# Second passes of overfull expert pairs in two branches, and four modulation groups of the second layer moved behind the first layer's experts

## The chip, the cores and the metric

The kernel runs on one core of a Trainium2 chip. The metric is the time of one execution on the device in microseconds (us); lower is better. The core has a matrix engine (PE, whose weight loads are listed as PEld), a vector engine (DVE), an activation engine (ACT), a general engine (POOL) and a queue that issues most transfers (SP). The engines run their own instruction streams and meet at semaphores. The program has real branches: each engine reads a register and jumps or falls through.

## What is computed

Two layers of a trunk over 512 latent and 256 context tokens of width 1024. Each layer begins with a modulation vector of six parts from the conditioning vectors, normalises and modulates its input, projects it, runs four mixers, projects back, and ends in a mixture of 32 experts. Each token goes to two experts of one group. Cut to what matters here:

```python
for layer in range(DEPTH):                                    # DEPTH = 2
    m_lat = split((c_act @ w_mod[layer] + b_mod[layer]), 6)   # w_mod[layer]: 1024 x 6144
    m_ctx = split(c_ctx_act @ w_mod[layer] + b_mod[layer], 6)
    h = rmsnorm(x) * (1 + scale1) + shift1                    # shift1, scale1: the first two of the six parts
    x = x + gate1 * (mixers(h @ w_in[layer]) @ w_out[layer])
    h = rmsnorm(x) * (1 + scale2) + shift2
    for e in range(32):                                       # each token: two experts of one group
        gu = h[tokens of e] @ w_gu[e]                         # 1024 x 512
        y = (silu(gu[:, :256]) * gu[:, 256:]) @ w_dn[e]       # 256 x 1024
    x = x + gate2 * weighted sum of the two y of a token
```

## The kernel before

**Modulation.** The 6144 outputs are computed in 12 groups of 512. `modulation` (L326) issues for one group two small loads of the bias and two loads of 1 MB of `w_mod`, does 64 matmuls of 128x32 by 128x128 with the conditioning vectors `cT`, adds the bias into `mr` and, for groups 0 to 3, transposes it and copies it into the table `AB` from which the first norm of the layer is modulated. The first layer's groups 0 to 3 are computed at the kernel's start. Its groups 4 to 11 and then groups 0 to 3 of the second layer are yielded by `mods` (L1431) into the last weave of the first layer's mixers. A weave takes turns among generators of program pieces by the shares in `STEPS`; this one holds a recurrence, an attention and `mods`, whose share is the last number of `STEPS[0]`. The second layer's weave holds its own groups 4 to 11.

**Experts.** Experts are handled in 16 pairs, one expert on each half of the partitions. A pair needs six pieces of weights of 1 MB: four of `w_gu` and two of `w_dn`. They are loaded by SP into 18 slots (`wslot`), in turn, and `prefetch` orders a piece as soon as its slot can be reused; a rule "few at a time" (`DEEP` = 4) makes each piece wait until the fourth one before it has landed. For a pair, `block_up` does 32 matmuls (`mm<-w,xT`) and the activation `ac`; `into` transposes the next pair's gathered tokens (`pt`); `block_down` transposes the activation (`po`) and does 16 matmuls (`sc<-w,aT`); `weighted` applies the gates; `scatter` adds the rows to the stream `XA` in memory by an indirect transfer of POOL. Where one expert of a pair has more than 64 tokens, a branch (L2038) behind `weighted` does a second pass, up and down, from the same weights. The register `cregs[p_]` tells which: 0 none, 1 or 2 one half of the pair (`half_swapped`), 3 or more both halves and another gather (`swapped`). So the weights of a pair can only be released behind this branch.

**Between the layers.** A last branch (L2052) holds a loop for experts that are still more overfull. An engine that passes this branch waits at its end for its own outstanding transfers, SP for those of all its eight semaphores. Behind it, `norm1` of the second layer loads six tiles `xn` of the stream (L473), squares each on ACT (L481), forms the reciprocal root on ACT as an exponential of a logarithm (L300, L301), scales on DVE (L487), transposes on PE (L498), modulates on ACT into `htmp` (L505), and splits into a high and a low part on DVE. Chunks of `w_in` (L522) are split likewise, the high part on ACT (L527), the low one on DVE (L531). The projection's matmuls (`pj<-h,w`) need both. A scheduler orders each engine's instructions at build time, so they are not always in the order of the code.

## Time and profile before

| quantity | value |
|---|---|
| time, median of 3 runs | 1741.66 us (1739.35 to 1742.36) |
| time of the profiled execution | 1741.17 us |
| its span, first to last instruction | 1739.4 us |
| mean granted clock of PE | 0.938 |
| busy: PE, DVE, ACT, POOL | 1447.7, 700.0, 536.6, 338.8 us |
| moved by transfers | 366 MB |

The span is 1.8 us shorter than the profiled execution's time. Busy times are unions of an engine's instructions, and the shares differ much between stages: first layer's mixers to about 507 us, its experts from 640 to 915, second layer from 922, its experts from 1455 to 1717. A position "at 656.67" is the time from the span's start.

### The profile page before, as it was taken

To read this page: it belongs to the slowest core of one execution; us is meant where nothing else is said; L and a number is where in the kernel's file an instruction comes from. 1 tells how busy PE (TensorE), PEld (TensorE's weight loads), DVE (VectorE), ACT (ScalarE), POOL (GpSimd) and SP (SyncE) were. 2 spreads that over 40 slices of the span, in tenths; PEclk is the share of its full clock that TensorE was granted. 3 is DMA by queue.
4 is the path that set the end of the run, shared out by engine and by line. 5 is a ranking of instruction groups with operands and counts; after the bars stand their busy time and mean duration, and the time that the engine had idled before them with its cause. 6 is when DMAs were issued, how large, how long until landed. Compare 5 with 4: busy or idle time off the path is not lost. (4 is left out here: it accounts for less than half of the span.)

```text
span 1739.4 us, 26685 instructions
## 1 busy us (share of the span) xinstructions
PE 1447.7 (83%) x10515; PEld 985.1 (57%) x10515; DVE 700.0 (40%) x1415; ACT 536.6 (31%) x1086; POOL 338.8 (19%) x262
## 2 busy tenths in 40 slices
PE   6999999989889848887885989999787775887883
PEld 4888778746669823322234978677366672332221
DVE  5263353477733452211114452635876244111111
ACT  5342453464422220100004442624743121100001
POOL 0022121120102233554430020301111122111100
PEclk9999989999999969999997999989898897999997
DMA  9332411057548599999985332211533598999996
GB/s 319 95 117 69 125 57 34 33 190 245 174 149 230 164 385 327 382 373 386 372 297 144 98 89 72 75 31 56 165 127 119 190 308 328 381 347 368 379 382 236
DMA packets 179833, 366.01 MB, mean 210 GB/s; under 512 B 39673, under 2 KB 90529, under 8 KB 179361
## 3 DMA queue, kind: packets, MB, share of 16 engines
q1 hardware_dynamic: 167440, 335.54, 54.7%
q0 software_dynamic: 9216, 20.99, 4.8%
q10 hardware_dynamic: 2960, 6.58, 1.0%
q8 instruction: 138, 2.26, 0.5%
q14 instruction: 79, 0.64, 0.1%
HBM read 338.48 MB, written 39.65 MB: 217 GB/s over the span
## 5 line engine op out<-in xcount | busy, mean ns | idle before, releaser
L297 PE MATMUL mm<-w,xT 128*64 128x512 f32 (+1 forms) x1120 | 269.5, 591 | 31.8 <-DMA w<-in_moe_w_gu_dram 13.3
L297 PE MATMUL pj<-h,w 128*128 128x256 f32 (+1 forms) x1224 | 228.2, 342 | 0.5 <-DVE u L945 0.3
L297 PEld LDWEIGHTS pj<-h,w 128*128 128x128 f32 x1224 | 190.0, 192 | 28.7 <-issue 5.2
L297 PEld LDWEIGHTS mm<-w,xT 128*64 128x64 f32 x1120 | 89.2, 139 | 188.0 <-issue 138.5
L297 PE MATMUL sc<-w,aT 128*64 128x512 f32 x536 | 131.5, 600 | 19.5 <-ACT aT L1953 16.5
L297 PE MATMUL pj<-w,h 128*128 128x256 f32 x864 | 118.3, 294 | 0.0
L297 PEld LDWEIGHTS pj<-w,h 128*128 128x128 f32 x864 | 111.4, 199 | 3.8 <-issue 3.1
L2013 POOL DMA_INDIRECT XA<-yes,row x32 | 50.9, 1590 | 305.3 <-DVEq L2038 254.1
L1943 ACT ACTIVATE ac<-mm 128x256 f32<-128x256 f32 x32 | 12.3, 383 | 312.0 <-PE mm L297 312.0
L1944 DVE TENSOR_TENSOR ac<-ac,mm 128x256 f32<-128x256 f32 x32 | 13.5, 421 | 226.2 <-ACT ac L1943 226.2
L297 PE MATMUL mm<-w,h 128*128 128x256 f32 x624 | 84.2, 296 | 14.0 <-PEq L1526 6.4
L531 DVE TENSOR_TENSOR w<-w 128x2048 fp32r<-128x2048 f32 (+1 forms) x26 | 58.0, 2230 | 91.3 <-ACT w L527 91.3
L297 PEld LDWEIGHTS sc<-w,aT 128*64 128x64 f32 x536 | 42.3, 136 | 85.7 <-issue 54.7
L297 PEld LDWEIGHTS mm<-w,h 128*128 128x128 f32 x624 | 80.8, 203 | 14.7 <-issue 6.6
L1624 POOL TENSOR_TENSOR xh<-xc,gr 128x512 f32<-128x512 f32 (+1 forms) x25 | 30.2, 1208 | 194.2 <-DVE xc L1620 89.7
L297 PE MATMUL sc<-h 128*128 128x256 f32 (+3 forms) x144 | 60.2, 535 | 8.8 <-ACT um L1221 7.8
L1927 PEld LDWEIGHTS pt<-masks,xgr 128*128 128x128 f32 x256 | 28.8, 147 | 68.1 <-issue 68.1
L1927 PE MATMUL pt<-masks,xgr 128*128 128x128 f32 x256 | 40.7, 293 | 31.5 <-DMA xgr<-XG,row 18.0
L527 ACT ACTIVATE w<-w 128x2048 fp32r<-128x2048 f32 (+1 forms) x26 | 48.0, 1847 | 60.6 <-PE pj L297 36.8
L297 PE MATMUL x<-u 64*32 64x32 f32 (+5 forms) x944 | 54.0, 251 | 12.0 <-DVE u L785 9.6
L297 PE MATMUL sc<-h,w 128*128 128x512 f32 (+1 forms) x312 | 59.4, 350 | 0.3 <-ACT ux L300 0.3
L297 PEld LDWEIGHTS x<-u 64*64 64x64 f32 (+4 forms) x944 | 45.4, 146 | 24.3 <-issue 9.1
(399 smaller groups left out, 2367.8 us busy)
## 6 DMA issues: line engine op xcount, KB each, us to landing
w<-in_moe_w_gu_dram SPq DMA_DIRECT2D x128, 1024.0 KB
w<-in_moe_w_dn_dram SPq DMA_DIRECT2D x64, 1024.0 KB
w<-in_w_mod_dram SPq DMA_DIRECT2D x40, 1024.0 KB
w<-in_w_in_dram SPq DMA_DIRECT2D x22, 1024.0 KB
wm<-in_w_mod_dram SPq DMA_DIRECT2D x8, 1024.0 KB
XG<-xh ACTq DMA_DIRECT2D x10, 512.0 KB
w<-in_w_out_dram SPq DMA_DIRECT2D x8, 512.0 KB
w<-in_w_out_dram SPq DMA_DIRECT2D x16, 256.0 KB
```

The lines of the kernel that those rows point to most:

```text
L297: TE.matmul(o, lhsT, rhs, start=start, stop=stop, **kw)
L527: sp = S.activation(hi[:, :, 0:o], raw[:, :, 0:o], AF.Copy)
L531: V.tensor_tensor(lo[:, :, 0:o], raw[:, :, 0:o], hi[:, :, 0:o].bitcast(F32), op=ALU.subtract)
L1624: G.tensor_tensor(xh[:, t0 - qt0:t0 - qt0 + m].rearrange("p n (e c q) -> p c n q e", e=2, c=4)[:, c], xs.rearrange(pairs, e=2), bc(gr[:, 1 ...
L1927: TE.transpose(pt[:, u * P:(u + 1) * P], xg[:, o:o + P], ident)
L1943: S.activation(ac[rs_], pm[rs_, 0:256], AF.Silu)
L1944: V.tensor_tensor(ac[rs_], ac[rs_], pm[rs_, 256:512], op=ALU.mult)
L2013: G.indirect_dma_start(out=XA, out_offset=bass.IndirectOffsetOnAxis(ap=row, axis=0), in_=ye, in_offset=None, bounds_check=T - 1, oob_is_er ...
```

## The change

The four groups of the second layer leave `mods`, and the share of `mods` in that weave goes from 12 to 8. The function `mod_ahead` loads them at the end of the first layer's expert loop: when the loop comes to its last two pairs it takes nine more of the expert slots, one for the four groups' biases (cleared by DVE, filled by eight small loads) and eight for the weights. The matmuls are done behind the last branch (now L2094) by `drain(modulation(...))`. Secondly, the second pass of an overfull pair stands in two branches: its up part directly behind `block_up`, its down part where the whole pass stood. Its activations are kept in `yes` buffers between the two. The diff, cut to its core:

```diff
-STEPS = ((38, 24, 60, 18, 12, 12, 66, 72, 12), (38, 24, 60, 18, 12, 12, 66, 72, 8))
+STEPS = ((38, 24, 60, 18, 12, 12, 66, 72, 8), (38, 24, 60, 18, 12, 12, 66, 72, 8))
...
-    def modulation(L, gs, slot=None, bank=None):
+    def mod_bias(L, g, bt):
+        for w in range(2):
+            nc.sync.dma_start(bt.rearrange("(j r) c -> j r c", r=32)[:, w, :],
+                              a["b_mod"][L, g * 512:(g + 1) * 512].rearrange("(j c) -> j c", j=4))
+    def mod_weights(L, g, kh, wt):
+        nc.sync.dma_start(wt, a["w_mod"][L, kh * 512:(kh + 1) * 512, g * 512:(g + 1) * 512].rearrange("(k p) c -> p k c", p=P))
+    def modulation(L, gs, slot=None, bank=None, there=None):
...
-            bt = bmt[i_ % 4]
-            for w in range(2):
-                nc.sync.dma_start(bt.rearrange("(j r) c -> j r c", r=32)[:, w, :], a["b_mod"][L, cs].rearrange("(j c) -> j c", j=4))
+            bt = there[g][2] if there else bmt[i_ % 4]
+            if not there:
+                mod_bias(L, g, bt)
...
-                    wt = (slot or ring)([P, 4, 512])
-                    nc.sync.dma_start(wt, a["w_mod"][L, k * P:(k + 4) * P, cs].rearrange("(k p) c -> p k c", p=P))
+                    if there:
+                        wt = there[g][k // 4]
+                    else:
+                        wt = (slot or ring)([P, 4, 512])
+                        mod_weights(L, g, k // 4, wt)
                 for j in range(4):
                     mm(pm[32 * j:32 * j + 32, 0:P], cT[:, k, :], wt[:, k % 4, j * P:(j + 1) * P], k == 0, k == KT - 1)
...
         def mods():
             yield from modulation(L, range(4, 12))
-            if not last:
-                yield from modulation(L + 1, range(4))
         weave((hgrn_, st[6]),
               (chain(mla_qkv(Em, hu, cs, c2, mw, mr_), restore(Ex), mla(Em, mr_)), st[7]), (mods(), st[8]))
...
+        ahead = {}
+        def mod_ahead(g):
+            if not ahead:
+                bs = wslot()
+                V.memset(bs[:, 0:512], 0.0)
+                for g_ in range(4):
+                    ahead[g_] = [None, None, bs[:, g_ * P:(g_ + 1) * P]]
+                    mod_bias(L + 1, g_, ahead[g_][2])
+            for kh in range(2):
+                ahead[g][kh] = wslot().rearrange("p (k c) -> p k c", k=4)
+                mod_weights(L + 1, g, kh, ahead[g][kh])
...
-        def half_swapped(p_, wh, xT, ye, gt, h):
+        def half_up(wh, xT, ac, h):
...
+        def half_down(p_, wh, ac, ye, gt, h):
...
+        def overfull(c_, first, second, more):
+            with tc.If(c_ > 0):
+                with tc.If(c_ < 2) as c1_:
+                    first()
+                with c1_.Else():
+                    with tc.If(c_ < 3) as c2_:
+                        second()
+                    with c2_.Else():
+                        more()
...
         xT = block_in(xgs[0], None, (S.copy, S.copy))
         for p_ in range(NP):
             prefetch(max(0, min(6 * p_ + NW, 3 * NEXP) - len(loaded)), False)
+            for g in () if last else range(4):
+                if 6 * p_ + NW >= 3 * NEXP + 2 * g + 3 and (not ahead or ahead[g][0] is None):
+                    mod_ahead(g)
             w_ = pair(p_)
             xT_, ac = xT, block_up(w_, xT)
+            a2, a3 = (yes[:, (p_ + i) % YE, 0:256] for i in (1, 2))
+            def more_up():
+                block_up(w_[::-1], xT_, ac=a2)
+                gather(yes[:, (p_ + 2) % YE], tab(1, p_, "row"))
+                block_up(w_, into(p_, 1, xT_), ac=a3)
+            def more_down():
+                swapped(p_, w_, a2, ye, gt)
+                y1 = block_down(w_, block_act(a3))
+                scatter(weighted(p_ + 1, y1, gates_of(tab(1, p_, "own")), tab(1, p_, "gws")), tab(1, p_, "row"))
             if p_ == 0:
                 slot_weights(ohs, tabs[0])
                 slot_weights(slot_table(wk, 1, tabs[1]["row"]), tabs[1])
+            overfull(cregs[p_], lambda: half_up(w_[0], xT_, a2, 1), lambda: half_up(w_[1], xT_, a2, 0), more_up)
             rows(p_ + NG)
             if p_ + 1 < NP:
                 xT = into(p_ + 1)
             gt = gates_of(tab(0, p_, "own"))
             ye = weighted(p_, block_down(w_, block_act(ac)), gt, tab(0, p_, "gws"))
-            with tc.If(cregs[p_] > 0):
-                with tc.If(cregs[p_] < 2) as c1_:
-                    half_swapped(p_, w_[0], xT_, ye, gt, 1)
-                with c1_.Else():
-                    with tc.If(cregs[p_] < 3) as c2_:
-                        half_swapped(p_, w_[1], xT_, ye, gt, 0)
-                    with c2_.Else():
-                        swapped(p_, w_, xT_, ye, gt)
-                        gather(yes[:, (p_ + 2) % YE], tab(1, p_, "row"))
-                        y1 = block_down(w_, block_act(block_up(w_, into(p_, 1, xT_))))
-                        scatter(weighted(p_ + 1, y1, gates_of(tab(1, p_, "own")), tab(1, p_, "gws")), tab(1, p_, "row"))
+            overfull(cregs[p_], lambda: half_down(p_, w_[0], a2, ye, gt, 1), lambda: half_down(p_, w_[1], a2, ye, gt, 0), more_down)
             scatter(ye, tab(0, p_, "row"))
...
-            pieces[0] = 6
+            pieces[0] = 6 if last else 3 * NEXP + 9
...
                     scatter(weighted(b, y1, gates_of(g_.get("own")), g_["gws"]), g_["row"])
+        if not last:
+            drain(modulation(L + 1, range(4), None, pmm, ahead))
         ec.close()
```

On SP, the last pieces of the first layer's experts and what follows them. Before, the last pieces are two `w_dn` loads; a wait for `DMAHW1` is one for the landing of the latest transfer on that one of SP's eight semaphores, which it uses in turn:

```order
L1465 DMA w_15411<-in_moe_w_gu_dram 128x2x1024 [waits DMAHW1_49,PE_49]
L1465 DMA w_15413<-in_moe_w_gu_dram 128x2x1024 [waits DMAHW2_49,PE_49]
L1470 DMA w_15415<-in_moe_w_dn_dram 128x2x1024 [waits DMAHW3_49]
L1470 DMA w_15417<-in_moe_w_dn_dram 128x2x1024 [waits DMAHW4_49]
L2038 COMPARE_AND_BRANCH
```

After them SP came to the branch L2052. In the changed kernel the same four pieces of the last pair (the last `w_dn` with the wait for `DMAHW4`, the fourth transfer before it; in turn it uses `DMAHW0` itself) are followed by one of the pair's branches and then by these rows, where `w_15450` is the slot of the biases:

```order
L328 DMA w_15450<-in_b_mod_dram 4x128 [waits DVE_49,PE_49]
L328 DMA w_15450<-in_b_mod_dram 4x128 x3
L328 DMA w_15450<-in_b_mod_dram 4x128 [waits DMAHW5_49]
L328 DMA w_15450<-in_b_mod_dram 4x128 [waits DMAHW6_49]
L328 DMA w_15450<-in_b_mod_dram 4x128 [waits DMAHW7_49]
L328 DMA w_15450<-in_b_mod_dram 4x128 [waits DMAHW0_49]
L332 DMA w_15460<-in_w_mod_dram 128x4x512 [waits DMAHW1_49]
```

A further branch follows, and then:

```order
L332 DMA w_15462<-in_w_mod_dram 128x4x512 [waits DMAHW2_49]
L332 DMA w_15464<-in_w_mod_dram 128x4x512 [waits DMAHW3_49]
L332 DMA w_15466<-in_w_mod_dram 128x4x512 [waits DMAHW4_49,PE_49]
L332 DMA w_15688<-in_w_mod_dram 128x4x512 [waits DMAHW5_49]
L332 DMA w_15690<-in_w_mod_dram 128x4x512 [waits DMAHW6_49,PE_49]
L332 DMA w_15692<-in_w_mod_dram 128x4x512 [waits DMAHW7_49]
L332 DMA w_15694<-in_w_mod_dram 128x4x512 [waits DMAHW0_49,PE_49]
L2094 COMPARE_AND_BRANCH
```

What moved: eight small loads and eight of 1 MB stand between the last expert piece and the last branch, and the eighth small load waits for `DMAHW0`. Behind the last branch SP went on before with:

```order
L2052 UNCONDITIONAL_BRANCH [waits DMAHW0_49,DMAHW1_49,DMAHW2_49,DMAHW3_49,DMAHW4_49,DMAHW5_49,DMAHW6_49,DMAHW7_49]
L522 DMA w<-in_w_in_dram 128x8x64 [waits DMASW4_49,DMASW5_49,DMASW0_49,DMASW7_49,DVE_49,DMAHW1_49,PE_49,Pool_49]
L522 DMA w<-in_w_in_dram 128x8x32 [waits DMAHW2_49]
L522 DMA w<-in_w_in_dram 128x8x32 [waits DMAHW3_49]
L473 DMA xn_17222<-XA 128x1024 [waits DMAHW4_49,DMASW3_49]
L473 DMA xn_17229<-XA 128x1024 [waits DMAHW5_49]
L522 DMA w<-in_w_in_dram 128x8x256 [waits DMAHW6_49]
L473 DMA xn_17237<-XA 128x1024 [waits DMAHW7_49]
```

and now with:

```order
L2094 UNCONDITIONAL_BRANCH [waits DMAHW0_49,DMAHW1_49,DMAHW2_49,DMAHW3_49,DMAHW4_49,DMAHW5_49,DMAHW6_49,DMAHW7_49]
L484 DMA xn_17208<-XA 128x1024 [waits DMAHW1_49,DMASW7_49,DMAHW2_49,DMASW3_49,PE_49]
L484 DMA xn_17215<-XA 128x1024 [waits DMAHW3_49,PE_49]
L484 DMA xn_17223<-XA 128x1024 [waits DMAHW4_49,PE_49]
L484 DMA xn_17231<-XA 128x1024
L484 DMA xn_17339<-XA 128x1024 [waits DMAHW5_49]
L533 DMA w<-in_w_in_dram 128x8x64 [waits DMASW5_49,DMASW7_49,DMASW1_49,DMAHW6_49,DVE_49,Pool_49]
L533 DMA w<-in_w_in_dram 128x8x32 [waits DMAHW7_49]
L533 DMA w<-in_w_in_dram 128x8x32 [waits DMAHW0_49]
L484 DMA xn_17347<-XA 128x1024 [waits DMAHW1_49]
L533 DMA w<-in_w_in_dram 128x8x256 [waits DMAHW2_49,PE_49]
```

What moved: the tiles of the stream `xn` stand ahead of the chunk of `w_in`; the wait at the branch's end is the same in form.

On ACT, the start of the second layer. Before:

```order
L527 ACTIVATE w<-w 128x8x128 [waits DMAHW5_49,DMAHW3_49,DMAHW7_49,DMAHW2_49,DMAHW1_49]
L191 ACT_TABLE_LOAD
L481 ACTIVATE junk,ss<-xn_17222 128x1024 [waits DMAHW4_49,DMAHW6_49,DMAHW0_49,PE_49]
L300 ACTIVATE ss<-ss,eps 128x1 [waits Activation_49]
L481 ACTIVATE junk,ss<-xn_17229 128x1024 [waits DMAHW5_49]
L301 ACTIVATE ss<-ss 128x1 [waits Activation_49]
L300 ACTIVATE ss<-ss,eps 128x1 [waits Activation_49]
L301 ACTIVATE ss<-ss 128x1 [waits Activation_49]
L527 ACTIVATE w<-w 128x2048 [waits DMAHW6_49,Pool_49]
L481 ACTIVATE junk,ss<-xn_17237 128x1024 [waits DMAHW7_49]
L505 ACTIVATE htmp<-mm,AB_150 128x256 [waits PE_49]
```

In the changed kernel ACT begins the second layer with the same squares, and these are the first rows and those that follow on them:

```order
L492 ACTIVATE junk,ss<-xn_17208 128x1024 [waits DMAHW3_49,DMAHW2_49,DMAHW4_49,DMAHW1_49,DMAHW6_49,DMAHW0_49,PE_49]
L300 ACT_TABLE_LOAD
L300 ACTIVATE ss<-ss,eps 128x1 [waits Activation_49]
L492 ACTIVATE junk,ss<-xn_17215 128x1024 [waits DMAHW2_49]
L301 ACT_TABLE_LOAD
L301 ACTIVATE ss<-ss 128x1 [waits Activation_49]
L300 ACT_TABLE_LOAD
L300 ACTIVATE ss<-ss,eps 128x1 [waits Activation_49]
L492 ACTIVATE junk,ss<-xn_17223 128x1024 [waits DMAHW3_49]
L301 ACT_TABLE_LOAD
L301 ACTIVATE ss<-ss 128x1 [waits Activation_49]
L300 ACT_TABLE_LOAD
```

```order
L300 ACTIVATE ss<-ss,eps 128x1 [waits Activation_49]
L492 ACTIVATE junk,ss<-xn_17231 128x1024 [waits DMAHW4_49]
L301 ACT_TABLE_LOAD
L301 ACTIVATE ss<-ss 128x1 [waits Activation_49]
L516 ACTIVATE htmp<-mm,AB_150 128x256 [waits DMAHW7_49,DMAHW5_49,PE_49]
L516 ACTIVATE htmp<-mm,AB_150 128x256 [waits PE_49] x3
L516 ACTIVATE htmp<-mm,AB_150 128x256 [waits DVE_49,PE_49,Activation_49] x2
L300 ACT_TABLE_LOAD
L300 ACTIVATE ss<-ss,eps 128x1
L516 ACTIVATE htmp<-mm,AB_150 128x256 [waits DVE_49,PE_49,Activation_49]
L538 ACTIVATE w<-w 128x8x128 [waits DMAHW6_49,DMAHW7_49,DMAHW5_49,DMAHW0_49]
```

What moved: the first `htmp` stands behind four squares and six table loads, one for each change between L300 and L301, where there was one table load before; the split of `w_in` (now L538, followed by one more table load) stands behind seven `htmp`, where it stood first.

On PE, one pair's branch. Before, behind the down matmuls, with the up and the down part inside:

```order
L297 MATMUL sc<-w_14237,aT 64x512
L2016 TENSOR_LOAD cnti
L2038 COMPARE_AND_BRANCH
L2039 COMPARE_AND_BRANCH
L297 MATMUL mm<-w_14227,xT 64x256 x8
L297 MATMUL mm<-w_14231,xT 64x256 x8
L1951 MATMUL po<-masks,ac 128x64 x2
L297 MATMUL sc<-w_14235,aT 64x512 x4
L2039 UNCONDITIONAL_BRANCH
```

In the changed kernel the first branch of a pair, behind its up matmuls, and the second one, behind its down matmuls:

```order
L297 MATMUL mm<-w_15222,xT 64x512
L297 MATMUL mm<-w_15224,xT 64x512
L2053 TENSOR_LOAD cnti
L2038 COMPARE_AND_BRANCH
L2039 COMPARE_AND_BRANCH
L297 MATMUL mm<-w_15218,xT 64x256 x8
L297 MATMUL mm<-w_15222,xT 64x256 x8
```

```order
L297 MATMUL sc<-w_15226,aT 64x512
L297 MATMUL sc<-w_15228,aT 64x512
L2038 COMPARE_AND_BRANCH
L2039 COMPARE_AND_BRANCH
L1975 MATMUL po<-masks,yes 128x64 x2
L297 MATMUL sc<-w_15226,aT 64x512 x4
L2039 UNCONDITIONAL_BRANCH
```

What moved: a pair has two branches to pass. By the code, a pair without a second pass jumps over 152 matmuls and their weight loads before, and over 104 and then 48 now.

## Rows read from the trace of the kernel before

**Rows 1.** The page's head and TensorE's busy time.
```profile
span 1739.4 us, 26685 instructions
...
PE 1447.7 (83%) x10515; PEld 985.1 (57%) x10515; DVE 700.0 (40%) x1415; ACT 536.6 (31%) x1086; POOL 338.8 (19%) x262
```

**Rows 2.** Windows; us, busy (count) of five engines, clock, DMA share, GB/s.
```profile
5.00:30.00 25.00, 14.66 (x179) 10.42 (x179) 13.21 (x47) 16.51 (x44) 0.00 (x0) 1.00 1.04 337
426.00:507.00 81.00, 72.53 (x963) 53.87 (x961) 48.70 (x111) 35.05 (x85) 7.67 (x6) 0.98 0.46 155
650.00:658.00 8.00, 7.45 (x53) 3.58 (x51) 2.88 (x9) 0.48 (x2) 1.08 (x1) 1.00 0.25 64
668.00:684.00 16.00, 13.31 (x60) 4.78 (x58) 2.62 (x4) 1.34 (x3) 12.41 (x6) 0.89 0.99 328
700.00:900.00 200.00, 162.11 (x724) 61.96 (x722) 33.24 (x51) 16.73 (x38) 92.36 (x45) 0.99 1.03 378
1462.00:1474.00 12.00, 10.88 (x76) 4.57 (x74) 3.88 (x16) 1.34 (x3) 2.48 (x2) 1.00 0.39 131
```

**Rows 3.** Windows, matmuls with cT alone; us, busy of PE, PEld, DVE.
```profile
426.00:507.00 81.00, 12.54 (x384) 10.12 (x384) 0.00 (x0) 0.98 0.46 155
```

**Rows 4.** Timeline of SP, start of the first layer's experts.
```profile
656.67 5.83 SPq L1465 DMA_DIRECT2D w<-in_moe_w_gu_dram  x4
...
676.50 2.82 SPq L1465 DMA_DIRECT2D w<-in_moe_w_gu_dram  x4
```

**Rows 5.** Timeline of PE there.
```profile
640.76 7.45 PE L297 MATMUL mm<-w,xT 128*64 128x512 f32 x30
...
654.74 3.62 PE L297 MATMUL mm<-w,xT 128*64 128x256 f32 x32
...
676.68 8.71 PE L297 MATMUL mm<-w,xT 128*64 128x512 f32 x32 [2.17 <-PEq L2038]
```

**Rows 6.** Line of the branch of the second pass; ns min/median/max.
```profile
L2038 PEldq COMPARE_BRANCH  x32: 65/3036/4998, 651.7 to 1713.0; - x32
...
L2038 POOLq INC_SWDGE_SEM  x29: 307/942/1415, 672.9 to 1701.6; - x29
```

**Rows 7.** Timeline of PE, start of the second layer's experts.
```profile
1457.15 7.60 PE L297 MATMUL mm<-w,xT 128*64 128x512 f32 x32
```

**Rows 8.** Timeline of SP there.
```profile
1471.50 1.40 SPq L1465 DMA_DIRECT2D w<-in_moe_w_gu_dram  x3
```

**Rows 9.** Line of the last branch; ns min/median/max.
```profile
L2052 SPq EVENT_SEMAPHORE  x16: 3/17/17, 906.0 to 1712.9; - x16
```

**Rows 10.** Waits of SP between the layers; us, times, longest.
```profile
SPq L522 <- remote: 15.5, 1, 15.5
SPq L2052 <- SPq L2052: 9.4, 1, 9.4
```

**Rows 11.** Timeline of SP between the layers.
```profile
922.43 1.78 SPq L522 DMA_DIRECT2D w<-in_w_in_dram  x3
924.32 1.27 SPq L473 DMA_DIRECT2D xn<-XA  x2
```

**Rows 12.** Timeline of SP at the kernel's start.
```profile
22.50 1.30 SPq L332 DMA_DIRECT2D bmt<-in_b_mod_dram  x2
```

**Rows 13.** Timeline of ACT between the layers.
```profile
927.39 1.06 ACT L527 ACTIVATE w<-w 128x1024 fp32r<-128x1024 f32 x1 [16.91 <-DMA w<-in_w_in_dram]
928.46 1.28 ACT L191 ACT_TABLE_LOAD   x1
929.90 1.06 ACT L481 ACTIVATE junk<-xn 128x1024 f32<-128x1024 f32 x1 [0.16 <-DMA xn<-XA]
...
931.09 0.29 ACT L300 ACTIVATE ss<-ss,eps 128x1 f32<-128x1 f32 x1
...
936.97 0.55 ACT L505 ACTIVATE htmp<-mm,AB 128x256 f32<-128x256 f32 x1
```

**Rows 14.** Timeline of PE there.
```profile
939.90 1.42 PE L297 MATMUL pj<-h,w 128*128 128x256 f32 x5
```

More of the change, by code (lines that the diff above doesn't have):

```diff
@@ L1929, in block_in, with block_up @@
             return xT
+        ahead = {}
[9 more added lines that the diff above has]
+                mod_weights(L + 1, g, kh, ahead[g][kh])
         def span(hv):
             return slice(64 * hv[0], 64 * hv[-1] + 64)
-        def block_up(w_, xT, hv=(0, 1)):
+        def block_up(w_, xT, hv=(0, 1), ac=None):
             pm = pmm()
@@ L1940, in block_up @@
                     mm(pm[hs, :], xT[:, k, hs], w_[h][k // 4][:, k % 4, :], k == 0, k == KT - 1)
-            ac = wk.tile([P, 256], F32, name="ac", tag="ac", bufs=1)
+            if ac is None:
+                ac = wk.tile([P, 256], F32, name="ac", tag="ac", bufs=1)
             rs_ = span(hv)
@@ L1982, in weighted, with swapped @@
             return ye
-        def swapped(p_, w_, xT, ye, gt):
-            y2 = weighted(p_ + 1, block_down(w_[::-1], block_act(block_up(w_[::-1], xT))), gt, tab(0, p_, "swp"))
+        def swapped(p_, w_, ac, ye, gt):
+            y2 = weighted(p_ + 1, block_down(w_[::-1], block_act(ac)), gt, tab(0, p_, "swp"))
             V.tensor_tensor(ye, ye, y2, op=ALU.add)
-        def half_swapped(p_, wh, xT, ye, gt, h):
+        def half_up(wh, xT, ac, h):
             hs, other = span([h]), span([1 - h])
@@ L1995, in half_swapped @@
                     mm(pm[ps, 0:256], xT[:, k, hs], wh[k // 4][:, k % 4, c * 256:(c + 1) * 256], k == 0, k == KT - 1)
-            ac = wk.tile([P, 256], F32, name="ac", tag="ac", bufs=1)
             S.activation(ac[hs], pm[other, 0:256], AF.Silu)
             V.tensor_tensor(ac[hs], ac[hs], pm[hs, 0:256], op=ALU.mult)
+        def half_down(p_, wh, ac, ye, gt, h):
+            hs, other = span([h]), span([1 - h])
             aT = block_act(ac, (h,))
```

## Prediction

> **What bounds the kernel now.** I read the page first: PE is busy for 1447.7 of 1739.4 us [rows 1], so over the whole run PE work taken away looks like time won. That share is a mean over stages, so I next asked for windows, one for each stage that the change touches, and compared in each PE's busy time with the share and rate of the transfers [rows 2]. The last weave of the first layer (426 to 507 us) has PE busy for 72.53 of 81 us and transfers at 0.46: PE nearly sets its pace. The first layer's experts (700 to 900 us) have transfers at a share of 1.03 and 378 GB/s, while PE is busy for 162.11 of 200 us: the loading of weights sets the pace there, and PE work or PE waits in it cost nothing so long as PE keeps up. Two short windows within the expert stages show transfers nearly idle: 650 to 658 us at 64 GB/s, and 1462 to 1474 us at 131 GB/s, while PE is busy in both. There the queue has nothing to load, because no slot is free. Last I followed SP, ACT and PE through the gap between the layers [rows 9 to 14], where PE waits for the stream's tiles and then for ACT's chain until its dense stretch begins at 939.90.
>
> **1. Work taken out of the weave.** Six groups of modulation are done in 426 to 507 us: 384 matmuls with 12.54 us of PE [rows 3], so 2.09 us for a group and 8.4 us for the four that leave. If PE set the pace alone, 8.4 us would be won; if the recurrence beside it did, nothing. PE's share there is 72.53/81 = 0.90, near the first end, and 0.90 x 8.4 = 7.5; I take 6.5, since the shorter queue at the weave's end has less to fill waits with. The eight loads that leave are cover for nothing (share 0.46). **-6.5 (0 to -8.4).**
>
> **2. Slots free earlier at the start of the first layer's experts.** Pair 0's up matmuls end at 640.76 + 7.45 = 648.2 [rows 5], but the first refill is issued at 656.67 [rows 4], because the second pass of this pair (32 matmuls, 654.74, 3.62 us) reads the same weights behind the down matmuls. Now it follows the up directly: 648.2 + 3.6 and about 1 us of activation, then the branch's end, so about 653, 3.7 us earlier. At 378 GB/s as the full rate, the window 650 to 658 lost 8 x (1 - 64/378) = 6.6 us. The window 668 to 684 lost 16 x (1 - 328/378) = 2.1 us: there SP gave out no load until 676.50, when PE had passed the branch of pair 1 (PE waits 2.17 us for it at 676.68). The up of a pair ends some 7 us before that branch, so this second hole should close. I take 3.7 + 2.1, **-6 (-3 to -8.7, all of both holes).** Since transfers pace the rest of the stage, the earlier stream carries through to its end.
>
> **3. The same in the second layer.** Pair 0's up ends at 1457.15 + 7.60 = 1464.75 [rows 7], the first refill is issued at 1471.50 [rows 8], and the window 1462 to 1474 lost 12 x (1 - 131/378) = 7.8 us. No second pass is taken there; with up to 2 us for the added branch the refill goes out at about 1467. **-4.5 (-2 to -7.8).**
>
> **4. The start of the second layer.** This is the dear part, in two steps.
>
> *The stream's tiles.* Before, SP passes the branch when the last expert piece has landed: it comes there at 896.6, waits 9.4 us, and its first semaphore comes at 906.0 [rows 9, 10]. It then waits 15.5 us more for the scatters, and issues at 922.43 the chunk of `w_in` and at 924.32 the tiles [rows 11]; the first square begins at 929.90 [rows 13]. Now eight bias loads and eight weight loads stand on SP ahead of the branch. The eighth bias load uses the semaphore of the last expert piece, so it waits until that has landed, and all the weight loads are queued behind it. So none of the 8.39 MB moves beside the experts. From 906.0 (all in the time of before; part 2's gain shifts both): a bias load takes 1.30/2 = 0.65 us to issue [rows 12], which puts the first weight load at 906.75. A tile takes 929.9 - 924.3 = 5.6 us to land with about 1 MB moved by then, which at 378 GB/s is 2.8, so some 2.8 us are latency. The loads take 8.39 MB at 378 (expert pieces) to 337 GB/s (5 to 30 us, mostly loads of `w_mod`) [rows 2], 22.2 to 24.9, I take 23.5; and 1.5 for the last pair's scatter that shares them. That is 906.75 + 2.8 + 23.5 + 1.5 = 934.5. SP waits for all of it at the branch's end, and only then issues the tiles, which land 4 us later (they now go first; between 1.4 us for 0.5 MB alone and 5.6): 938.7 instead of 929.9, **+8.8**.
>
> *ACT's chain.* Before, the split of the first chunk of `w_in` is done ahead of the tiles (927.39, 1.06 us, then a table load of 1.28); the first `htmp` comes at 936.97 and PE is dense at 939.90, 10.0 us after the first square [rows 13, 14]. Now ACT has, from the first square on: four squares with read-out at 931.09 - 929.90 = 1.2 us, six small operations at some 0.25, six table loads of 1.28, together 14.0; then seven `htmp` at 0.5 (0.55 less overlap), another table load and a small operation, 1.5, the split, 1.06, and DVE's half of it, about as long, 1.2: 7.3. So 21 us instead of 10, **+11**. The four groups' matmuls (8.4 us of PE) run while the weights land and in this chain, and cost nothing; uncovered they would add 8.4.
>
> Together **+20 (+14 to +24)**: the low end has tiles 3 us sooner and 3 us of the chain overlapped, the high end the slow rate and the full 5.6 us of landing.
>
> **5. More branches.** A pair passes two. On the engines other than PE a branch takes some 50 ns; POOL's bookkeeping at it takes 0.94 us in the median and up to 1.42 towards the end [rows 6], and the last scatter is on the path to the end. I take **+1.5 (0 to +2.5)**.
>
> **Sum.** -6.5 - 6 - 4.5 + 20 + 1.5 = +4.5 on the profiled execution's 1741.2, so 1745.7; that execution lies 0.5 below the median of the runs, and I say **1746**. All ends at once give 1730 to 1762.
>
> **Rivals.** *The holes close and the gap hides more (faster).* If transfers run on without a hole in both expert stages, parts 1 to 3 give 8.4 + 8.7 + 7.8 = 25, and the sum is 1741.2 - 25 + 20 + 1.5 = 1738; with the low end of part 4, 1732. For it: PE is ahead of the weights in both starts. Against: the slots of the down weights still wait for the down part, and the first four of six pieces last only some 10 us. It decides from 17 us won in parts 1 to 3 and a part 4 under 14.
>
> *The sum is nil (same).* The terms of both signs are of one size, so 3 us less in part 4, or more in parts 1 to 3, gives 1739 to 1745.
>
> *Both branches stall PE (much slower).* PE's branch takes 3.04 us in the median and up to 5.0 [rows 6], the others' some 50 ns. In 700 to 900 us PE works 162.11 of 200, so 13.8 of a pair's 17 us (six pieces of 1.05 MB at 378 GB/s are 16.6). One stall is covered: of pair 1's, PE sat idle for 2.17 [rows 5]. Two would leave it idle for 4.4, or for 6 with less queued behind it, so 18 to 20 us for a pair: 1.5 to 3 us over, in the 16 of 32 pairs above the median +24 to +48, 1770 to 1794. Against: a jump is now over 104 or 48 matmuls, not 152, and the shortest branch took 65 ns. The Trainium skill ("Runtime: NRT & Kernel Launch", "Instruction fetch mechanics") says that a taken branch stalls when its target is outside a window of two pages of 256 instructions; with their weight loads the jumps are 304 instructions before and 208 and 96 now, so by it stalls become rarer, and the sum stays.
>
> *Table switches cost more than their row (slower).* If the engine empties at each of the seven added switches ahead of the first projection for as long as a load takes, part 4 is +29 and the time 1755. Against: the load at 928.46 begins as the split ends, and the square behind it starts at 929.90 after 0.16 us of idle, put down to the tile [rows 13]; that is 1.28 with no room for more. The Trainium skill ("ScalarE: Activation LUTs", "What ACT_TABLE_LOAD costs") gives 1283 ns and a drain of 1380 ns for every switch, by which the time would be 1755; this trace shows the first and not the second.
>
> **How the numbers follow.** About 0.2%, 3.5 us, is what a measurement of this kernel tells from no change: 1738.2 to 1745.1 is "same". Forecast (slower, 1745 to 1758): 0.39. Nil: 0.28. Faster: 0.25. Stalls 0.04, dear switches 0.04. So faster 0.25, same 0.28, slower 0.47. The range leaves out the stalls, the lowest fifth or so of the faster case and the high end of part 4: 1733 to 1758; the likeliest case alone has 1745 to 1758.
>
> **What would show it.** Right: four groups fewer in 426 to 507; refills at about 653 and 1467 in place of 656.67 and 1471.50 (less what the weave gave); the first added load of `w_mod` issued only as the last `w_dn` lands; the first square 9 us later after that landing than before, PE dense 21 us after the square. Wrong: weight loads of `w_mod` beside the last experts, tiles issued before all of them have landed, holes that stay where they are, or a PE branch above 2 us twice in a pair with transfers falling under 370 GB/s.

## The result, and the profile after

The changed kernel takes 1756.03 us (median of 4 runs, 1751.90 to 1756.32) against 1741.26 for the kernel before (4 runs): a ratio of 1.0074, 95% interval 1.0053 to 1.0096, so 0.7% slower. The forecast was 1746, slower, with 1733 to 1758 as the range. The profiled execution grew from 1741.17 to 1756.09, by 14.9 where the sum of the prediction says +4.5.

The page's head and PE's busy time, as in [rows 1]; PE is busy for 13.5 us more, though it does the same 10515 matmuls, at a mean granted clock of 0.920 in place of 0.938:

```profile
span 1754.2 us, 27020 instructions
...
PE 1461.2 (83%) x10515; PEld 1009.0 (58%) x10515; DVE 702.7 (40%) x1416; ACT 545.0 (31%) x1093; POOL 339.2 (19%) x262
```

To find where the time went I cut every profiled execution at the same six events of its timelines: A, from the start to the first up matmul of the first layer's pair 0; B, to the end of the last down matmul there; C1, to ACT's first square of the second layer; C2, to the 121st projection matmul `pj`; D, to the first up matmul of the second layer; E, to the end. In us (an ordinary table, worked out from starts and ends in the timelines; the experiments stand in it too):

| kernel | A | B | C1 | C2 | D | E | span |
|---|---|---|---|---|---|---|---|
| before | 639.9 | 274.4 | 15.7 | 29.3 | 498.0 | 282.2 | 1739.4 |
| after | 628.7 | 270.7 | 26.8 | 44.3 | 501.0 | 282.5 | 1754.2 |
| e1_split_only | 637.9 | 269.3 | 16.4 | 27.9 | 496.5 | 281.6 | 1729.6 |
| e2_ahead_only | 631.4 | 282.4 | 24.9 | 42.7 | 500.0 | 282.7 | 1764.1 |
| e3_table_once | 626.9 | 269.4 | 28.3 | 44.4 | 495.5 | 283.7 | 1748.2 |
| e4_bias_early | 630.6 | 296.2 | 16.7 | 29.4 | 492.5 | 281.6 | 1747.1 |
| e5_in_order | 631.7 | 277.0 | 22.3 | 29.5 | 498.0 | 281.3 | 1739.8 |
| e6_two_groups | 637.5 | 277.1 | 16.2 | 28.6 | 494.7 | 283.2 | 1737.3 |
| e7_chunks_first | 624.2 | 271.6 | 40.6 | 32.2 | 494.2 | 282.1 | 1744.9 |
| e8_quarter_loads | 631.3 | 268.8 | 13.1 | 44.8 | 499.6 | 277.9 | 1735.5 |
| e9_groups_left_out | 632.0 | 276.4 | 15.7 | 28.7 | 498.8 | 340.7 | 1792.4 |

Each row is one execution. Kernels with the same code in a stage differ there: A by up to 7.8 us (624.2 to 632.0), D by 8.5, E by 2.4 (without e8 and e9, which do other work there). So small differences count only where several rows agree.

After against before: A wins 11.2, B 3.7; C1 loses 11.1, C2 15.0, D 3.0, E nothing. So the loss is the gap between the layers, C1 and C2, 26.1 us.

*The gap, SP.* The timeline of SP there, which answers to [rows 9 to 11] (start, us, then operation, tile and count):

```profile
881.76 10.04 SPq L328 DMA_DIRECT2D w<-in_b_mod_dram  x8
891.84 18.14 SPq L332 DMA_DIRECT2D w<-in_w_mod_dram  x8
922.40 2.26 SPq L484 DMA_DIRECT2D xn<-XA  x5
924.90 6.18 SPq L533 DMA_DIRECT2D w<-in_w_in_dram  x3
931.12 0.96 SPq L484 DMA_DIRECT2D xn<-XA  x1
932.19 25.81 SPq L533 DMA_DIRECT2D w<-in_w_in_dram  x2
```

Its waits, and the windows that go with them (us, busy and count of PE, PEld, DVE, ACT, POOL, granted clock, DMA share, GB/s):

```profile
SPq L2094 <- SPq L2094: 11.6, 1, 11.6
```

```profile
638.89:646.89 8.00, 6.91 (x56) 4.01 (x54) 2.10 (x9) 1.33 (x3) 1.08 (x1) 1.00 0.47 164
656.89:672.89 16.00, 14.01 (x66) 5.84 (x64) 2.67 (x5) 1.31 (x3) 12.55 (x7) 1.00 1.02 368
885.00:892.00 7.00, 7.00 (x34) 2.32 (x34) 2.73 (x3) 0.58 (x1) 1.45 (x2) 1.00 0.38 144
900.00:922.00 22.00, 10.79 (x239) 8.49 (x243) 1.81 (x9) 0.00 (x0) 1.58 (x1) 0.84 0.95 332
939.00:957.00 18.00, 12.54 (x55) 9.99 (x55) 11.22 (x25) 15.86 (x30) 0.00 (x0) 0.59 0.00 1
945.73:970.57 24.84, 22.59 (x144) 21.22 (x144) 11.48 (x27) 13.03 (x28) 0.00 (x0) 0.79 0.15 43
1476.48:1488.48 12.00, 10.00 (x70) 4.17 (x68) 3.38 (x16) 1.34 (x3) 0.99 (x1) 1.00 0.60 210
```

The eight bias loads hold SP for 10 us. The first load of `w_mod` goes out at 891.84; the transfers run nearly dry before it (885 to 892 at 144 GB/s) and carry the 8.39 MB behind it (900 to 922 at 332). SP waits 11.6 us at the branch's end for all of it, and only then, at 922.40, issues the tiles.

*The gap, ACT and PE.* The timelines of ACT and of PE, answering to [rows 13, 14]:

```profile
926.25 1.06 ACT L492 ACTIVATE junk<-xn 128x1024 f32<-128x1024 f32 x1 [30.59 <-DMA xn<-XA]
...
927.42 1.28 ACT L300 ACT_TABLE_LOAD   x1
928.71 0.29 ACT L300 ACTIVATE ss<-ss,eps 128x1 f32<-128x1 f32 x1
...
939.79 2.89 ACT L516 ACTIVATE htmp<-mm,AB 128x256 f32<-128x256 f32 x6
...
944.64 1.04 ACT L538 ACTIVATE w<-w 128x1024 fp32r<-128x1024 f32 x1
...
952.09 0.37 ACT L1280 COPY ux<-pj 128x256 f32<-128x256 f32 x1 [2.04 <-PE pj L297]
...
953.36 1.92 ACT L538 ACTIVATE w<-w 128x2048 fp32r<-128x2048 f32 x1
```

```profile
945.73 0.80 PE L297 MATMUL pj<-h,w 128*128 128x256 f32 x2 [0.47 <-ACT w L538]
946.99 5.06 PE L297 MATMUL pj<-h,w 128*128 128x256 f32 x22 [0.47 <-DVE w L542]
951.85 2.12 PE L509 MATMUL mm<-masks,xn 128*128 128x128 f32 x9
955.33 0.74 PE L297 MATMUL pj<-h,w 128*128 128x256 f32 x4 [1.36 <-ACT w L538]
```

The first `pj` comes 945.73 - 926.25 = 19.5 us after the first square. Before, it came 8.7 us after it (929.90), as PE's timeline and the window up to the 121st `pj` there show:

```profile
938.61 0.79 PE L297 MATMUL pj<-h,w 128*128 128x256 f32 x2
```

```profile
938.61:959.17 20.56, 20.42 (x153) 19.64 (x151) 12.19 (x37) 12.98 (x34) 0.00 (x0) 0.90 0.16 52
```

PE then does 24 `pj` and stands again at 955.33, for the split of the second chunk of `w_in`. That chunk was ordered at 932.19, 9.8 us after the first tile; before it was 1.3. But it isn't the chunk that is late: from 939 to 957 the transfers run at 1 GB/s, so it had landed by then. ACT splits it only at 953.36, behind a copy of the first products (`ux`, 952.09) for which it waits 2.04 us for PE. From the first to the 121st `pj` it takes 24.84 us, before 20.56: PE is idle for 2.25 us in place of 0.14, and busy for 22.59 in place of 20.42, at a mean granted clock of 0.79 in place of 0.90.

*The expert stages.* PE's and SP's timelines at the two starts, answering to [rows 4, 5, 7, 8]; the first line is of the kernel before, where the window of [rows 5] cut off the first two of the 32 matmuls:

```profile
639.85 8.36 PE L297 MATMUL mm<-w,xT 128*64 128x512 f32 x32
```

```profile
628.74 8.57 PE L297 MATMUL mm<-w,xT 128*64 128x512 f32 x32
...
640.07 3.67 PE L297 MATMUL mm<-w,xT 128*64 128x256 f32 x32 [0.24 <-issue]
...
1471.63 8.67 PE L297 MATMUL mm<-w,xT 128*64 128x512 f32 x32
```

```profile
642.05 3.04 SPq L1474 DMA_DIRECT2D w<-in_moe_w_gu_dram  x4
...
1483.50 2.44 SPq L1474 DMA_DIRECT2D w<-in_moe_w_gu_dram  x3
```

The first refill goes out 642.05 - 628.74 = 13.3 us after the first up matmul (656.67 - 639.85 = 16.8 before) and 1483.50 - 1471.63 = 11.9 in the second layer (14.4 before). In windows at the same distance from the first up matmul as those of [rows 2], the hole of 64 GB/s has become 164, that of 131 has become 210, and the 328 at pair 1 has become 368. So the first holes are shorter, not closed.

### The profile page after: what moved, and what is told of

Same layout as the page of the kernel before. It is cut to its first block, busy times and chain, and to the rows that moved or that the text cites. A ratio compares the mean times of both kernels' runs of the same rounds, so it can differ in the third digit from the quotient of the medians.

```text
span 1754.2 us, 27020 instructions
## 1 busy us (share of the span) xinstructions
PE 1461.2 (83%) x10515; PEld 1009.0 (58%) x10515; DVE 702.7 (40%) x1416; ACT 545.0 (31%) x1093; POOL 339.2 (19%) x262
## 5 line engine op out<-in xcount | busy, mean ns | idle before, releaser
L297 PE MATMUL mm<-w,xT 128*64 128x512 f32 (+1 forms) x1120 | 286.9, 598 | 28.7 <-DMA w<-in_moe_w_gu_dram 23.8
L297 PEld LDWEIGHTS mm<-w,xT 128*64 128x64 f32 x1120 | 98.2, 141 | 202.1 <-issue 154.9
L297 PE MATMUL sc<-w,aT 128*64 128x512 f32 x536 | 135.9, 626 | 12.3 <-ACTq L2038 9.0
L1968 DVE TENSOR_TENSOR ac<-ac,mm 128x256 f32<-128x256 f32 x32 | 13.4, 420 | 241.6 <-ACT ac L1967 241.6
L297 PEld LDWEIGHTS sc<-w,aT 128*64 128x64 f32 x536 | 47.3, 143 | 75.1 <-issue 54.5
L297 PEld LDWEIGHTS mm<-w,h 128*128 128x128 f32 x624 | 81.0, 203 | 14.4 <-issue 6.2
L1853 POOL DMA_INDIRECT xgr<-XG,row x32 | 34.5, 1079 | 175.5 <-PE po L1975 98.6
L538 ACT ACTIVATE w<-w 128x2048 fp32r<-128x2048 f32 (+1 forms) x26 | 48.0, 1847 | 41.4 <-PE pj L297 37.1
L297 PEld LDWEIGHTS x<-u 64*32 64x32 f32 (+4 forms) x944 | 46.6, 151 | 24.3 <-issue 15.2
L1936 PE MATMUL pt<-masks,xgr 128*128 128x128 f32 x256 | 37.7, 293 | 21.9 <-DMA xgr<-XG,row 18.3
```

Of the source, the lines that this page charges most:

```text
L297: TE.matmul(o, lhsT, rhs, start=start, stop=stop, **kw)
L538: sp = S.activation(hi[:, :, 0:o], raw[:, :, 0:o], AF.Copy)
L1853: return G.indirect_dma_start(out=xg, out_offset=None, in_=XG, in_offset=bass.IndirectOffsetOnAxis(ap=row, axis=0), bounds_check=T - 1, oo ...
L1936: TE.transpose(pt[:, u * P:(u + 1) * P], xg[:, o:o + P], ident)
L1968: V.tensor_tensor(ac[rs_], ac[rs_], pm[rs_, 256:512], op=ALU.mult)
```

## The experiments

The edits are shown against the changed kernel, that of e9 against the kernel before. Times are medians, ratios are to the kernel before on the same chip.

**One part at a time.** First the split branches without the groups behind the experts:

```diff
-STEPS = ((38, 24, 60, 18, 12, 12, 66, 72, 8), (38, 24, 60, 18, 12, 12, 66, 72, 8))
+STEPS = ((38, 24, 60, 18, 12, 12, 66, 72, 12), (38, 24, 60, 18, 12, 12, 66, 72, 8))
...
             yield from modulation(L, range(4, 12))
+            if not last:
+                yield from modulation(L + 1, range(4))
...
-            for g in () if last else range(4):
-                if 6 * p_ + NW >= 3 * NEXP + 2 * g + 3 and (not ahead or ahead[g][0] is None):
-                    mod_ahead(g)
...
-        if not last:
-            drain(modulation(L + 1, range(4), None, pmm, ahead))
```

> The second passes split in two branches, the modulation left where it was. Theory (the loss lies between the layers, and the split pays a little in both expert stages): about 3.5 us won at the first layer's expert stage and 0 to 3 at the second's, so 1736 to 1740. Rival (the added branches, or the split, cost time themselves): 1745 or more.

Measured: 1733.12 us, ratio 0.9954 (0.9942 to 0.9967): faster, the best version of all, and better than both ranges. B is 5.1 us shorter than before, and in the window at the same distance from the first up matmul (648.08 to 656.08) the transfers run at 156 GB/s in place of 64. E is 0.6 shorter, which is nothing.

Then the groups behind the experts with the second pass in one branch, as before:

```diff
-            overfull(cregs[p_], lambda: half_up(w_[0], xT_, a2, 1), lambda: half_up(w_[1], xT_, a2, 0), more_up)
...
-            overfull(cregs[p_], lambda: half_down(p_, w_[0], a2, ye, gt, 1), lambda: half_down(p_, w_[1], a2, ye, gt, 0), more_down)
+            with tc.If(cregs[p_] > 0):
+                with tc.If(cregs[p_] < 2) as c1_:
+                    half_swapped(p_, w_[0], xT_, ye, gt, 1)
...
```

> The four groups moved behind the first layer's experts, one branch per pair as before. Theory: the weave wins about 11 us, the gap between the layers costs 22 to 26 more, and nothing of the split's gain is there, so 1755 to 1760. Rival (the loss comes from the split): about 1741 or less.

Measured: 1763.07 us, ratio 1.0104 (1.0062 to 1.0147). Its C1 and C2 are as long as in the changed kernel (67.6 against 71.1, before 45.0), so the loss in the gap belongs to the groups. The time is 3 us above the range of the theory. The two parts add up: 21.7 slower and 8.3 faster than the kernel before make 13.4, and the whole change has 0.74% of 1741, 12.9. The 8.5 us that A wins here are lost again in B (8.0 longer); why B is longer without a second branch was not followed further.

**ACT's chain.** One table load ahead of the squares in place of one at each change, and the splits after the third tile:

```diff
+                if n == 0:
+                    ln_exp(x_[0:1, 0:1])
+                fixed(S.activation(junk, x_, AF.Square, accum_out=ss))
...
+                if n == 2 and chunks:
+                    chunks()
...
-            ws_.append(wchunk(C2, first=True))
-            ln_exp()
-            ws_.append(wchunk([(C_G, 256)]))
-            norm1(E, hsplit, early)
+            norm1(E, hsplit, early, lambda: (ws_.append(wchunk(C2, first=True)), ws_.append(wchunk([(C_G, 256)]))))
```

> The changed kernel with one table load ahead of the first square in place of eight between squares, logarithms, exponentials and the split, and the split behind three squares; the loads of w_mod as they were. Theory (ACT's chain is on the path): the dense stretch of PE begins 8 to 11 us sooner behind the first square, 1745 to 1748. Rival (something else, such as the weights of w_in, ends the wait as late): 1754 to 1757.

Measured: 1753.50 us, ratio 1.0072 (1.0045 to 1.0100), against the kernel before the same as the change (1.0074), and just under the rival's range. ACT's chain did become short, but C2 stays at 44.4. PE's and ACT's timelines of this kernel and a window of it show where the time went:

```profile
934.82 0.51 PE L297 MATMUL pj<-h,w 128*128 128x256 f32 x2 [0.62 <-ACT w L542]
...
936.31 4.24 PE L297 MATMUL pj<-h,w 128*128 128x256 f32 x22 [0.71 <-DVE w L546]
942.82 0.80 PE L297 MATMUL pj<-h,w 128*128 128x256 f32 x2 [2.27 <-ACT w L542]
945.15 4.87 PE L297 MATMUL pj<-h,w 128*128 128x256 f32 x22 [1.53 <-DVE w L546]
952.88 1.69 PE L513 MATMUL mm<-masks,xn 128*128 128x128 f32 x6 [2.86 <-DVE xn L502]
```

```profile
940.59 0.37 ACT L1284 COPY ux<-pj 128x256 f32<-128x256 f32 x1 [5.37 <-PE pj L297]
940.86 1.91 ACT L542 ACTIVATE w<-w 128x2048 fp32r<-128x2048 f32 x1
```

```profile
936.00:941.00 5.00, 4.24 (x22) 4.04 (x22) 1.52 (x5) 0.41 (x2) 0.00 (x0) 0.66 0.00 0
```

The first `pj` comes 10.2 us after the first square (924.64) in place of 19.5. Then PE waits for the second chunk's two splits (2.27, 1.53) and for the next tile (2.86). The chunk is there again: nothing is moved from 936 to 941. Its split stands on ACT behind the copy `ux`, for which ACT waits 5.37 us until PE has done its first 24 `pj`. So a second wait in ACT's order takes the place of the first. C1 is no shorter (28.3).

The other order, both chunks split ahead of the squares:

```diff
+                ld = nc.sync.dma_start(xn[n], x_src(L, n))
+                if L:
+                    fixed(ld)
...
+                sq = S.activation(junk, x_, AF.Square, accum_out=ss)
+                if L:
+                    fixed(sq)
...
+                if first:
+                    fixed(ld)
...
-            ws_.append(wchunk([(C_G, 256)]))
+            ws_.append(wchunk([(C_G, 256)], first=True))
```

> The changed kernel with ACT held to the order of before at the second layer's start: both chunks' splits and the one table load ahead of the squares; SP still issues the tiles ahead of the chunks. Theory (in the changed kernel two things end late, ACT's chain by 10.7 us and the second chunk by 4.4 more): the splits wait for the second chunk, which lands some 12 us behind the first tile, then the dense stretch has no gaps; 3 to 6 us less, 1750 to 1753. Rival (ACT's order alone makes the 15 us): 1740 to 1743.

Measured: 1755.93 us, ratio 1.0061 (1.0037 to 1.0085), no better than the change within the intervals, and above both ranges. ACT's timeline:

```profile
930.36 1.06 ACT L544 ACTIVATE w<-w 128x1024 fp32r<-128x1024 f32 x1 [38.31 <-DMA w<-in_w_in_dram]
931.43 1.28 ACT L191 ACT_TABLE_LOAD   x1
934.59 1.91 ACT L544 ACTIVATE w<-w 128x2048 fp32r<-128x2048 f32 x1 [1.87 <-DMA w<-in_w_in_dram]
936.40 1.04 ACT L494 ACTIVATE junk<-xn 128x1024 f32<-128x1024 f32 x1
```

ACT now waits for both chunks to land and squares 10 us later; C2 is 32.2, C1 40.6, and their sum 72.8 (71.1 with the change). Here it is the chunks that are waited for (38.31 and 1.87 us): with SP's new order, tiles first, they land too late for ACT's old order. Where both SP and ACT have the order of before (e4, e5, e6) C2 is 28.6 to 29.5. SP's old order with ACT's new one was not tried.

**The bytes.** The `w_mod` loads of the four groups cut to a quarter, the rest cleared, so the modulation is another one:

```diff
-                mod_weights(L + 1, g, kh, ahead[g][kh])
+                wt = ahead[g][kh]
+                V.memset(wt[:, 1:4], 0.0)
+                nc.sync.dma_start(wt[:, 0], a["w_mod"][L + 1, kh * 512:kh * 512 + P, g * 512:(g + 1) * 512])
```

> The changed kernel with a quarter of each load of w_mod (256 KB of 1 MB; the rest of the slot is cleared, so the second layer's first norm is modulated from a part of the sum). Theory (between the layers the bytes count once the last scatter has landed): the tiles are issued some 13 us sooner, when the scatter lands, and ACT's chain stays; 1741 to 1745. Rival (the wait is for the branch or the bias loads, not for bytes): 1753 to 1757.

Measured: 1738.18 us, ratio 0.9956 (0.9930 to 0.9982). SP's timeline:

```profile
883.64 10.06 SPq L328 DMA_DIRECT2D w<-in_b_mod_dram  x8
893.74 10.03 SPq L1954 DMA_DIRECT2D w<-in_w_mod_dram  x8
909.45 2.78 SPq L484 DMA_DIRECT2D xn<-XA  x6
912.46 33.89 SPq L533 DMA_DIRECT2D w<-in_w_in_dram  x5
```

The tiles go out at 909.45, and C1 falls from 26.8 to 13.1; C2 stays at 44.8. So C1's loss is the bytes, and C2's is not: the order behind the branch is the same here. (With another modulation the second layer routes its tokens otherwise, here and in e9, so both are read in the first layer and the gap alone, and that this time lies under the theory's range says little.)

The four groups left out altogether from the kernel before (the share of `mods` again 8), the second layer modulated from the first one's table:

```diff
-            AB = ABs[L]
+            AB = ABs[0]
...
-            if not last:
-                yield from modulation(L + 1, range(4))
```

> The kernel before without the four groups at all: nothing loads or multiplies them, and the second layer's first norm is modulated from the first layer's table. What the weave alone can win. Theory (PE sets the weave's pace): 8 to 11 us, 1730 to 1733. Rival (the recurrence beside it sets the pace): 0 to 4 us, 1737 to 1741.

Measured: 1784.80 us, all of the loss in E (340.7), where more pairs are overfull (736 up matmuls in place of 512); its ratio says nothing here. A is 632.0, 7.9 less than before, and C1 and C2 are 15.7 and 28.7, as before. So the weave without the four groups is worth about 8 us, and taking them out of it does not by itself lengthen the gap.

**Loads beside the experts.** The biases first, so that the `w_mod` loads don't stand behind them, and these as early as their slots allow:

```diff
-            if not ahead:
-                bs = wslot()
...
+            ahead[g] = [None, None, bmt[g]]
...
+                with tc.high_priority():
+                    mod_weights(L + 1, g, kh, ahead[g][kh])
...
+        for g in () if last else range(4):
+            mod_bias(L + 1, g, bmt[g])
```

> The changed kernel with the four groups' biases loaded ahead of the expert loop into tiles of their own, so that the loads of w_mod follow the expert pieces without a wait for the last one; ACT's order at the second layer's start then comes out as before the change, with one table load. Theory (both the wait for the last piece and ACT's order count): tiles issued about 7 us sooner after the last piece and the dense stretch 10 us after the first square, together 16 to 18 us less, 1738 to 1740. Rival (the bytes of w_mod alone set the gap, whenever they are ordered): only ACT's part, 1745 to 1748.

Measured: 1754.27 us, ratio 1.0068 (1.0040 to 1.0096). The gap is as before (16.7 and 29.4), but B is 25.5 longer than with the change. PE's waits there:

```profile
PE mm L297 <- DMA w<-in_moe_w_gu_dram: 17.5, 4, 14.0
```

The modulation's weights went ahead of the last pair's, and PE waits 14.0 us for these at one place. B, C1 and C2 together are 342.3, with the change 341.8, so neither range holds. The next one gives the loads the rule "few at a time" of the expert pieces, so that they stand in line with them:

```diff
+                with tc.high_priority():
+                    ins = mod_weights(L + 1, g, kh, ahead[g][kh])
+                tc.add_manual_dep(ins.ins, started[-DEEP].ins.name, mybir.DependencyInfo(mybir.DependencyClass.Sync, mybir.DependencyReason.DATA),
+                                  reason="few at a time")
+                started.append(ins)
```

> The changed kernel with the biases loaded ahead of the loop and the eight loads of w_mod held to the rule of the expert pieces (each waits for the landing of the fourth before it), so that they follow the pieces without a hole and not ahead of the last pair's up weights; ACT's order at the second layer's start comes out as before the change. Theory (beside the experts each byte costs its time; only the time between the last piece and the tiles is free, some 20 us of the 24 that the loads take): tiles about 5 us later than with the split alone, the weave 9.5 us shorter, 1727 to 1732. Rival (the loads cost their full 24 us wherever they stand): 1744 to 1750.

Measured: 1740.93 us, ratio 0.9988 (0.9969 to 1.0008). SP's timeline, and a wait of PE:

```profile
886.50 2.83 SPq L332 DMA_DIRECT2D w<-in_w_mod_dram  x2
889.56 0.99 SPq L1479 DMA_DIRECT2D w<-in_moe_w_dn_dram  x2
898.26 15.48 SPq L332 DMA_DIRECT2D w<-in_w_mod_dram  x6
917.19 8.48 SPq L533 DMA_DIRECT2D w<-in_w_in_dram  x3
```

```profile
PE sc L297 <- DMA w<-in_moe_w_dn_dram: 3.1, 1, 3.1
```

Two of the eight loads still pass the last `w_dn`, and the other six stand behind it. C2 is 29.5, C1 22.3. Against the split alone, A wins 6.2 and B, C1 and C2 lose 7.7, 5.9 and 1.6. That is 15.2 us for 8.39 MB, less than the 24 of the rival and more than the 5 of the theory; the time is that of the kernel before. The same with groups 2 and 3 alone, 0 and 1 back in the weave:

```diff
-STEPS = ((38, 24, 60, 18, 12, 12, 66, 72, 8), (38, 24, 60, 18, 12, 12, 66, 72, 8))
+STEPS = ((38, 24, 60, 18, 12, 12, 66, 72, 10), (38, 24, 60, 18, 12, 12, 66, 72, 8))
...
+            if not last:
+                yield from modulation(L + 1, range(2))
...
+            for g in () if last else (2, 3):
...
+            drain(modulation(L + 1, (2, 3), None, pmm, ahead))
```

> As the one before, but only groups 2 and 3 are moved (four loads, 4.2 MB, 11 us); groups 0 and 1 stay in the weave. Theory (11 us fit into the free time between the last piece and the tiles): nothing lost there against the split alone, the weave about 4.7 us shorter, 1726 to 1731. Rival (each byte costs its time): the weave wins 4.7, the loads cost 11 to 12, 1738 to 1742.

Measured: 1739.05 us, ratio 0.9993 (0.9973 to 1.0012). The gap costs nothing here (16.2 and 28.6), but A is 637.5, no shorter than with the four groups in the weave (637.9), and B is 7.8 longer than with the split alone. The time is in the rival's range. A saving in proportion to the groups isn't seen, but A differs by as much between kernels with the same weave, so one execution doesn't exclude it.

## Why the prediction came out as it did

The direction, the gap as the cause, and the mechanism of the tiles and of ACT's chain were right; the sum is 10 us short. It would be further off if step 1 had not won 4.7 more than put: steps 2 to 4 and a stage outside the sum miss by some 16 the other way. The time lies near the upper end of a wide range, and the 1755 of the rival with dear table switches is nearer by chance, since its mechanism isn't in the trace. By the prediction's own steps:

**1, the weave: -6.5 put, -11.2 measured.** The eight kernels without the four groups in the weave have A at 629.6 in the mean, those with them (before and e1) at 638.9: 9.3 in place of 6.5. That is about PE's own work, 8.4, which the prediction had as the end of its range; taking only 0.9 of it and then less was too careful. The kernels lie up to 5.4 us from these means, so whether two groups win half of it (e6: nothing) isn't settled.

**2, the slots in the first layer: -6 put, -3.7 measured (-5.1 in e1).** The step was right in its mechanism, and nearly in its size. The refill came 16.8 - 13.3 = 3.5 us earlier against the first up matmul, where 3.7 was put. The hole at pair 1 closed (368 GB/s); the first one lost 8 x (1 - 164/378) = 4.5 us in place of 6.6, so 2.1 of the 3.7 put. That is 3.8 for both, about as B has it (3.7). Over more kernels it is more: the five with the split and no load of `w_mod` ahead of the last expert piece (after, e1, e3, e7, e8) have B at 270.0 in the mean, before and e9 at 275.4.

**3, the slots in the second layer: -4.5 put, nothing measured.** The refill did come 2.5 us earlier, and the hole lost 12 x (1 - 210/378) = 5.3 in place of 7.8. But E is no shorter: the seven kernels with the split and the same routing have it at 282.3 in the mean, before and e2 at 282.2 and 282.7. In the changed kernel the last two `w_dn` loads are issued from 241.8 us after the first up matmul on, before from 241.6: the gain is lost on the way. After the hole the transfers run at 369, 365 and 379 GB/s over 220 us, before at 368, 369 and 384, which accounts for about 1.5 of the 2.5 us (0.5 MB less at 372 GB/s). What slows them isn't settled. What failed is the size (the refill 11.9 us behind the first up matmul, where "about 1467" means 9.9), and above all that the earlier stream carries through to the stage's end, which was said for the first layer and held there.

**4, the gap: +20 put, +26.1 measured.** *Tiles, +8.8 put, +11.1.* As put: the eighth bias load waits for the last expert piece, `w_mod` moves only then, and the tiles behind the branch. From the last expert piece to the tiles' issue it is now 922.40 - 891.30 = 31.1 us, before 924.32 - 906.0 = 18.3 [rows 9, 11]; the eighth bias load was issued at 891.30. From the first `w_mod` load to the tiles' issue it takes 922.40 - 891.84 = 30.6, where 934.5 - 906.75 = 27.8 was put; at the 332 GB/s measured in 900 to 922, in place of the 357 in the 23.5 us put, 8.39 MB take 25.3, which is 1.8 of the 2.8 missing. With a quarter of the bytes (e8) C1 is 13.1. *ACT's chain, +11 put, +15.0 in C2.* The chain itself was sized well: from the first square to the first `pj` it is 19.5 us, before 8.7, so 10.8 against 11 put. What was not in the sum is the 4.3 us behind the first `pj`: 2.1 of PE's idle time, 1.36 of them for the split of the second chunk, and 2.2 of busy time at the lower granted clock. E3 shows that the first projections have a second wait in ACT's order, of about the length that the shorter chain wins; with the old order of SP and ACT (e4, e5, e6) both are gone. So of "ACT's chain costs 11" the cost holds, but not that a shorter chain would win it back.

**5, the branches: +1.5 put.** Not seen: e1, which has all of the added branches, loses 0.7 us in C1 and nothing in any other stage. A cost within B or E, where the earlier refill won less than put, isn't excluded.

**D, +3.0, was not in the sum.** Between the 121st `pj` and the second layer's experts the code is the same, and the kernels lie between 492.5 and 501.0 there. In this stage the mean granted clock was 0.89 after and 0.92 before, and PE was busy for 423.3 us in place of 416.8. After, e2 and e8, the three with the long chain on ACT, have 0.89 to 0.90 and 499.6 to 501.0 us; the eight others have 0.91 to 0.93 and 492.5 to 498.8. Over the whole run one execution of the changed kernel had 0.931 and took 1751.90, the others 0.920 to 0.924 and about 1756.1. So the clock goes with the 3 us; whether the change has a part in it isn't settled.

**The rivals.** That the holes close and the gap hides more didn't happen: the first hole of each layer got shorter, and the gap grew. PE's stalls at the branches didn't become the pace either. The line of the branch (ns min, median, max) in the changed kernel, as in [rows 6]:

```profile
L2038 PEldq COMPARE_BRANCH  x64: 70/340/6875, 639.8 to 1727.6; - x64
```

Its median went from 3036 to 340 ns, though single ones are longer than any before; 18 of 32 branches took over 2 us before, 9 of 64 now. This agrees with the rule of the Trainium skill that the prediction weighed ("Runtime: NRT & Kernel Launch", "Instruction fetch mechanics"): with shorter jumps, stalls are rarer. (The jumps of 152, and now 104 and 48, count a block's matmuls as the trace does and a half's as the code does. By the code alone it is 104, and now 72 and 32, so shorter all the same.) Table switches cost their row and no more: the load at 927.42 takes 1.28 and the operation behind it begins at 928.71. The drain of 1380 ns that the Trainium skill adds ("ScalarE: Activation LUTs", "What ACT_TABLE_LOAD costs") isn't seen here either.

## What to carry to other kernels

Work that moves to a stage paced by transfers is free only for its matmuls; its bytes are paid there or behind it. In the best place tried here (e5) 8.39 MB cost 15.2 us, in the others more. When loads are placed ahead of a branch at whose end the queue waits for all of its transfers, count them and everything that can only be ordered behind it. Look for the second limit behind the first before a chain is shortened, and before a load is called late, see whether it had landed: here an engine's order was the limit twice. Time the parts of a change apart: here one of two is worth 0.46% and the other costs 1.0%.
